# Four Strassen pairs per feed-forward in place of three, a longer lead, and plain weights split in one piece

## The chip, the cores and the metric

The kernel runs on one core of a Trainium2 chip. The metric is the device time of one execution in microseconds (us), as a median over runs. TensorE (PE) multiplies matrices, VectorE (DVE) and ScalarE (ACT) work element by element, GpSimd (POOL) takes small side jobs, and SyncE (SP) issues the transfers from device memory.

## The reference, cut to what matters

The program runs two transformer blocks of depth 2, one after the other, over a sequence of 256 tokens of width 1024 in float32. Each of the four layers has a feed-forward, a token mixer and another feed-forward, so there are eight feed-forwards:

```
def swiglu(x, w13, w2):                      # D_FF = 2816
    a, b = jnp.split(x @ w13, 2, axis=-1)
    return (jax.nn.silu(a) * b) @ w2

def swiglu_2(h, w_in, w_out):
    gu = h @ w_in
    g, u = jnp.split(gu, 2, axis=-1)
    return (jax.nn.silu(g) * u) @ w_out
```

The first block puts layer norms around feed-forwards and mixer (`x = layer_norm(ALPHA * x + 0.5 * swiglu(...))`), the second RMS norms. The mixers (gated recurrence and spatial gating in the first block, dilated attention and mLSTM in the second) are not touched by the change, but their weights pass through the same splitting code.

## The kernel before, in words

**Precision.** A float32 matrix is written as the sum of two reduced-precision matrices: a high part, which is a copy that rounds (ScalarE, line 268), and a low part, which is the matrix less its high part (VectorE, line 274; for 14 halves GpSimd, line 272). A product takes three matmuls: high by high, high by low, low by high (`mm3`, line 302, and line 547 in the pairs). `wh` and `wl` are the parts of a weight, `xh` and `xl` those of the activations.

**Units.** All weights come as one stream of units of 128 x 1024 numbers. A plain unit is loaded into the pool `stg` (four buffers) and split in two halves of 512 columns, each with one copy and one subtraction. `split(u)` splits all units up to number `u`, and `fetch` issues loads up to four units (`STAGES`) further. How far splitting runs ahead of TensorE's use in the order of the program is `lead()`: 2 to 5 units for plain ones, `PAIR` units where a product unit comes within `PAIR` units. A unit's two parts, and the loaded blocks of a pair, live in one ring of 24 buffers (`whp`, 2 x `RING`).

**The feed-forward.** The 2816 hidden columns are 11 groups of 256 (each group is one 512-column product: gate and value side by side), and the second matrix has 22 rows of units (`r`). The two halves of the tokens (i = 0 and 1) first do two groups (`OWN`) each by themselves. Then comes the joint part, in which every unit serves both halves (`joint`, the list `FFN`): `("g", n)` is one plain group, `("s", n, ...)` a pair of groups n and n + 1 by Strassen's products, with the rows named behind it done in the gaps, and `("r", k)` a row alone. After it each half does the six rows in `LAST`, and the norm follows.

**A pair.** Two groups by both token halves are a 2 x 2 block product. `pair` does it with seven products instead of eight. It loads four blocks in two units each (`raw`, lines 232 and 233). Seven operands are made from them, partly by adding blocks in place (`operand`, lines 245, 249 and 253, VectorE), and each operand is split 1024 columns at a time. On the way out of a pair ScalarE keeps four products (line 501), VectorE adds them (line 504) and multiplies by the gate (line 511), and the hidden rows are transposed and split (lines 294 and 295). A plain group instead ends in `hidden` (lines 440 to 451, 256 columns at a time).

**Order.** The order of instructions on TensorE, VectorE and ScalarE is set by a scheduler of the framework from the order of the program and its dependencies; SyncE and GpSimd keep the order of the program. Each engine works strictly in its order.

Of the kernel before, what the change touches and what calls it, by code (L numbers as in the profile page):

```python
# [11 lines left out]
F32 = mybir.dt.float32  # L12
# [7 lines left out]
P = 128  # L20
# [16 lines left out]
RAMP = 3  # L37
STEP = 1
TAIL = 2
PAIR = 5  # L40
LAGS = dict(ffn=9, mixer1=6, mixer2=6)
STAGES = 4
SLOTS = 31
# [10 lines left out]


OWN = 2
FFN = (("g", 8), ("s", 2, 0, 1, 2, 3), ("g", 9), ("s", 4, 16, 17, 4, 5), ("g", 10), ("s", 6, 6, 7, 18, 19),
       ("r", 8), ("r", 9), ("r", 20), ("r", 21))
LAST = (10, 11, 12, 13, 14, 15)


PRODUCTS = ("p1", "p2", "q5", "p3", "p6", "p7", "q4")
# [16 lines left out]
class Core:  # L79
# [125 lines left out]
    def lead(self):  # L205
# [3 lines left out]
        left = dict(ffn=len(_ffn_units()), mixer1=56, mixer2=36)[kind] - n  # L209
        if self.product(min(self.pos[0] + PAIR, self.nunit - 1)):  # L210
            return PAIR
        return LEAD + (MORE if n < FIRST else max(0, MORE - left // RAMP))
# [11 lines left out]
    def fetch(self, v):  # L224
        while self.next_dma <= min(v, self.nunit - 1):
            made = self.made[self.next_dma]
            if not self.product(self.next_dma):
                t = self.stages[self.next_dma] = self.stg.tile([P, 1024], F32, tag="stg", name=self.nm("stg"))
                for c in (slice(0, 512), slice(512, 1024)) if self.next_dma == 0 else (slice(0, 1024),):
                    self.nc.sync.dma_start(t[:, c], self.a["ws"][made][:, c])  # L230
            elif made[0] in LOADS:
                t = self.raw[made[:2]] = self.whp.tile([P, 1024], F32, tag="w", name=self.nm("raw"))
                self.nc.sync.dma_start(t, self.block(LOADS[made[0]], *made[1:]))
            self.next_dma += 1

# [3 lines left out]
    def operand(self, p, u, base):  # L239


        raw, add = self.raw, self.nc.vector.tensor_add
        if p in ("q5", "p6"):
            t = raw["p1", u]
            add(t, t, raw["q5" if p == "q5" else "p3", u])  # L245
            return t
        if p == "p7":
            t = raw.pop(("p3", u))
            add(t, t, raw.pop(("q5", u)))  # L249
            return t  # L250
        if p == "q4":
            t = raw.pop(("p1", u))
            add(t, t, raw.pop(("p2", u)))  # L253
            return t
        return raw[p, u]

    def split(self, u):
        while self.next_split <= min(u, self.nunit - 1):
            v = self.next_split
            self.fetch(v)  # L260
            made = self.made[v]
            product = self.product(v)
            w = self.operand(*made) if product else self.stages.pop(v)
            hi = self.whp.tile([P, 1024], F32R, tag="w", name=self.nm("wh"))
            lo = self.whp.tile([P, 1024], F32R, tag="w", name=self.nm("wl"))
            halves = [slice(0, 512), slice(512, 1024)]
            for h, c in enumerate([slice(0, 1024)] if product else halves):
                r = self.nc.scalar.activation(hi[:, c], w[:, c], AF.Copy)  # L268
                if v < 3:
                    self.pin(r)  # L270
                if h and self.pool_share(*self.phase[v]):
                    self.nc.gpsimd.tensor_tensor(lo[:, c], w[:, c], hi[:, c], op=ALU.subtract)
                else:
                    self.nc.vector.tensor_sub(lo[:, c], w[:, c], hi[:, c])  # L274
            self.units[v] = [hi[:, c] for c in halves], [lo[:, c] for c in halves]
            self.next_split += 1
            self.fetch(v + STAGES)
# [135 lines left out]
    def ffn(self, i, rs):  # L413
# [16 lines left out]
        while "done" not in J:  # L430
            yield 1
        yield from self.rows(i, range(len(LAST)), lambda n: J["h", i, LAST[n]], accs, None, len(LAST) - 1)
        return accs
# [23 lines left out]
    def joint(self, J, rs):  # L457

        for what, n, *ks in FFN:
            if what == "s":  # L460
# [1001 lines left out]
def _ffn_units():  # L1462


    out, n = list(range(4 * OWN)), 4 * OWN
    for what, _, *ks in FFN:
        if what == "s":
            base, gaps = n, GAPS[len(GAPS) - len(ks):]
            n += 8
            for p in PRODUCTS:  # L1470
                out += [(p, u, base) for u in range(2)]
                if p in gaps:
                    out.append(n)
                    n += 1
        else:
            m = 4 if what == "g" else 1
            out += range(n, n + m)
            n += m
    return out + list(range(n, n + len(LAST)))

# [15 lines left out]
def _ffn(w_in, w_out):  # L1496
    groups, w_out = _pairs(w_in), _rows(w_out)
    parts = [groups[:4 * OWN]]
    for what, n, *ks in FFN:
        if what == "s":  # L1500
            parts += [_blocks(w_in, n), w_out[list(ks)]]
        else:
            parts.append(groups[4 * n:4 * n + 4] if what == "g" else w_out[n:n + 1])
    return parts + [w_out[list(LAST)]]

# [94 lines left out]
```

## Time and profile before

| | before |
|---|---|
| median of 3 runs | 2171.57 us (2169.29 to 2174.26) |
| profiled execution | 2170.61 us, its span 2168.8 us |
| TensorE busy | 2116.2 us, 98% of the span |
| VectorE busy | 1879.8 us, 87% |
| ScalarE busy | 1352.0 us, 62% |
| GpSimd busy | 291.4 us, 13% |
| read from device memory | 391.63 MB, 181 GB/s over the span |

The span runs from the first instruction's start to the last one's end. Busy times are unions, so what overlaps on one engine counts once. Matmuls are pipelined and their ends are modelled: the rate of TensorE is better read from the starts of matmuls in a row than from its busy time.

### The profile page before, as it was taken

How to read it: one execution, taken by the hardware profiler on the slowest of the kernel's cores; microseconds unless marked ns; L12 is line 12 of the kernel's file. 1: busy time of each engine (PE TensorE's matmuls, PEld its weight loads, DVE VectorE, ACT ScalarE, POOL GpSimd, SP SyncE). 2: the span in 40 equal slices, each digit the busy share in tenths (PEclk: the TensorE clock that was granted, in tenths of full speed). 3: DMA queues.
4: the chain of work that ended last, by engine and by line, in shares of the span. 5: the costliest groups of instructions: out<-in, count | busy, mean ns of one | idle time of the engine just before them, and what ended most of it. 6: DMA issues, size and time to landing. Idle time of an engine off the chain costs nothing.

```text
span 2168.8 us, 28670 instructions
## 1 busy us (share of the span) xinstructions
PE 2116.2 (98%) x9968; PEld 1738.6 (80%) x9968; DVE 1879.8 (87%) x2837; ACT 1352.0 (62%) x2351; POOL 291.4 (13%) x319
## 2 busy tenths in 40 slices
PE   8999999999999999999999999999999999999998
PEld 6877888888788788888778787788778878788887
DVE  7998787899889879698989988689998998877995
ACT  6665755566566575565656665666666666576663
POOL 0000420000000033000100304610200010550000
PEclk9999999999999999999999999999999999999999
DMA  8547455455654655545555553434655546343552
GB/s 301 185 176 244 148 190 193 141 213 201 208 190 175 218 160 180 178 159 197 199 197 203 204 194 122 165 117 148 233 195 186 182 172 219 111 152 127 205 192 97
DMA packets 115296, 394.55 MB, mean 182 GB/s; under 512 B 12880, under 2 KB 15312, under 8 KB 115152
## 3 DMA queue, kind: packets, MB, share of 16 engines
q1 hardware_dynamic: 115152, 392.73, 52.5%
q8 instruction: 78, 1.28, 0.2%
q14 instruction: 66, 0.54, 0.1%
HBM read 391.63 MB, written 1.05 MB: 181 GB/s over the span
## 4 chain that ended last, share of the span: by engine, by line
PE 80%; DVE 10%; issue 3%; ACT 3%; POOL 2%; DMA 2%; SPq 0%; DVEq 0%; POOLq 0%; ACTq 0%
PE g L302 33%; PE big L302 23%; PE g L547 17%; DVE wl L274 5%; PE g L286 4%; ACT wh L268 2%; DMA stg<-in_ws_dram 2%; PE big L1262 1%; PE big L1291 1%; PE big L792 1%; DVE raw L245 1%; DVE kp L504 0%; DVE raw L249 0%; PE big L1209 0%; POOL cu L1135 0%
## 5 line engine op out<-in xcount | busy, mean ns | idle before, releaser
L274 DVE TENSOR_TENSOR wl<-stg,wh 128x512 fp32r<-128x512 f32 x1026 | 691.8, 708 | 129.6 <-ACT wh L268 123.3
L268 ACT ACTIVATE wh<-stg 128x512 fp32r<-128x512 f32 x1040 | 600.8, 623 | 200.8 <-PE g L302 83.8
L302 PE MATMUL g<-wh,xh 128*128 128x512 f32 x1184 | 483.1, 408 | 9.3 <-ACT wh L268 5.9
L302 PE MATMUL g<-wl,xh 128*128 128x512 f32 x1184 | 467.2, 395 | 0.5 <-DVE wl L274 0.5
L302 PE MATMUL g<-wh,xl 128*128 128x512 f32 x1184 | 465.3, 395 | 0.0
L268 ACT ACTIVATE wh<-raw 128x1024 fp32r<-128x1024 f32 x336 | 349.3, 1056 | 178.1 <-DVE raw L253 53.7
L274 DVE TENSOR_TENSOR wl<-raw,wh 128x1024 fp32r<-128x1024 f32 x336 | 410.2, 1236 | 25.1 <-ACT wh L268 23.1
L302 PEld LDWEIGHTS g<-wh,xh 128*128 128x128 f32 x1184 | 225.5, 190 | 58.8 <-ACT wh L268 7.3
L302 PEld LDWEIGHTS g<-wh,xl 128*128 128x128 f32 x1184 | 224.7, 190 | 50.4 <-DVE xl L311 2.0
L302 PEld LDWEIGHTS g<-wl,xh 128*128 128x128 f32 x1184 | 225.7, 191 | 43.4 <-DVE wl L274 1.8
L302 PE MATMUL big<-wh,hT 128*128 128x512 f32 x640 | 183.3, 390 | 0.0
L547 PE MATMUL g<-wh,Xh 128*128 128x512 f32 x384 | 149.7, 390 | 1.1 <-ACT kp L501 1.1
L547 PE MATMUL g<-wl,Xh 128*128 128x512 f32 x384 | 150.7, 393 | 0.0
L547 PE MATMUL g<-wh,Xl 128*128 128x512 f32 x384 | 150.2, 391 | 0.0
L302 PEld LDWEIGHTS big<-wh,hT 128*128 128x128 f32 x640 | 120.1, 188 | 25.3
L410 POOL TENSOR_TENSOR m<-m,nhalf 128x1 f32<-128x1 f32 (+1 forms) x24 | 23.1, 962 | 794.5 <-DVE m L409 794.5
L302 PE MATMUL big<-wh,hTh 128*128 128x512 f32 x384 | 124.8, 392 | 0.0
L302 PE MATMUL big<-wl,hTh 128*128 128x512 f32 x384 | 124.2, 390 | 0.0
L302 PE MATMUL big<-wh,hTl 128*128 128x512 f32 x384 | 124.0, 390 | 0.0
L245 DVE TENSOR_TENSOR raw<-raw,raw 128x1024 f32<-128x1024 f32 x96 | 120.6, 1268 | 0.5
L547 PE MATMUL g<-wh,xh 128*128 128x512 f32 x288 | 114.6, 398 | 1.4 <-ACT kp L501 1.4
L547 PE MATMUL g<-wl,xh 128*128 128x512 f32 x288 | 112.5, 391 | 0.0
(322 smaller groups left out, 3229.2 us busy)
## 6 DMA issues: line engine op xcount, KB each, us to landing
stg<-in_ws_dram SPq DMA_DIRECT2D x519, 512.0 KB, 4.4
raw<-in_ws_dram SPq DMA_DIRECT2D x192, 512.0 KB, 5.0
row<-in_norm_gain_dram SPq DMA_DIRECT2D x24, 256.0 KB, 6.8
row<-in_ln_g_dram SPq DMA_DIRECT2D x12, 256.0 KB, 4.9
row<-in_ln_b_dram SPq DMA_DIRECT2D x12, 256.0 KB, 6.3
xT<-in_xT_dram SPq DMA_DIRECT2D x4, 256.0 KB, 6.1
x<-in_x_dram SPq DMA_DIRECT2D x4, 256.0 KB, 8.7
out_dram<-x SPq DMA_DIRECT2D x4, 256.0 KB, 2.0
```

What stands on the lines that cost most here:

```text
L245: add(t, t, raw["q5" if p == "q5" else "p3", u])
L268: r = self.nc.scalar.activation(hi[:, c], w[:, c], AF.Copy)
L274: self.nc.vector.tensor_sub(lo[:, c], w[:, c], hi[:, c])
L286: self.nc.tensor.transpose(tp[:, hs(j)], src[:, hs(j)], self.ident)
L302: self.nc.tensor.matmul(accs[c], a, b[c], start=start and q == 0, stop=stop and q == 2)
L410: self.nc.gpsimd.tensor_tensor(out, out, self.nhalf[:, 0:n], op=ALU.pow)
L547: nc.tensor.matmul(bank[p], x[:, hs(k)], w[j], start=first[p] == p and k + q == 0, stop=k == 3 and q == 2, skip_group_check=True)
L792: nc.tensor.matmul(ps[:, 64 * h:64 * h + 64].rearrange("p (c m) -> p c m", m=m), Z[:, hs(h)], view(Z[:, hs(h)], m)[:, :, 1, :], start=True ...
L1262: nc.tensor.matmul(ps[:, hh * S + j * P:hh * S + j * P + P], J["aq", i][r, hs(head // 2)], J["ak", j][r, hs(head // 2)], start=True, stop= ...
L1291: nc.tensor.matmul(o[:, 64 * hh:64 * hh + 64], pT[:, hs(2 * hh + j)], J["av", j][:, head * 64:head * 64 + 64], start=j == 0, stop=j == 1)
```

## The change

Three edits. First, the list `FFN` has one plain group and four pairs one behind the other, where it had three groups and three pairs in turn; the rows are dealt out anew, and because two pairs now overlap in the stream, the loaded blocks are kept under a key with the pair's position (`base`) in it. Second, `PAIR` is 6 in place of 5. Third, a plain unit from number 8 on is split in one piece of 1024 columns, except the 14 units in the second mixers whose second half GpSimd splits.

```diff
-PAIR = 5
+PAIR = 6
...
-FFN = (("g", 8), ("s", 2, 0, 1, 2, 3), ("g", 9), ("s", 4, 16, 17, 4, 5), ("g", 10), ("s", 6, 6, 7, 18, 19),
-       ("r", 8), ("r", 9), ("r", 20), ("r", 21))
-LAST = (10, 11, 12, 13, 14, 15)
+FFN = (("g", 10), ("s", 2, 0, 1, 2, 3), ("s", 4, 20, 21, 4, 5), ("s", 6, 6, 7, 8, 9), ("s", 8, 10, 11, 12),
+       ("r", 13))
+LAST = (14, 15, 16, 17, 18, 19)
...
-                t = self.raw[made[:2]] = self.whp.tile([P, 1024], F32, tag="w", name=self.nm("raw"))
+                t = self.raw[made] = self.whp.tile([P, 1024], F32, tag="w", name=self.nm("raw"))
...
         if p in ("q5", "p6"):
-            t = raw["p1", u]
-            add(t, t, raw["q5" if p == "q5" else "p3", u])
+            t = raw["p1", u, base]
+            add(t, t, raw["q5" if p == "q5" else "p3", u, base])
             return t
...
-            for h, c in enumerate([slice(0, 1024)] if product else halves):
+            for h, c in enumerate([slice(0, 1024)] if product or v >= 8 and not self.pool_share(*self.phase[v]) else halves):
```

In the whole program the matmuls of 512 columns go from 8256 to 8160, the 1024-wide low parts of operands from 336 to 448, the operand sums from 192 to 256, and the low parts of plain units from 1026 instructions of 512 columns to 434 of 1024 and 30 of 512.

VectorE's order changes most behind a pair. This is VectorE before, in the third feed-forward, behind the last low part of its first pair; `stg` names a plain unit, `raw` a block or operand of a pair, `kp6` and `kp7` are kept products:

```order
L504 TENSOR_TENSOR kp6_1352_5721<-kp6_1352_5721,g_1334_5630 128x512
L274 TENSOR_TENSOR wl_1366_5789<-stg_1345_5686,wh_1365_5788 128x512
L511 SCALAR_TENSOR_TENSOR kp6_1352_5721<-kp6_1352_5721,kp1_1323_5580 128x512
L274 TENSOR_TENSOR wl_1366_5789<-stg_1345_5686,wh_1365_5788 128x512
L295 TENSOR_TENSOR hTl_1359_5750<-g_1357_5744,hTh_1358_5749 128x512
L504 TENSOR_TENSOR kp7_1364_5773<-kp7_1364_5773,kq5_1338_5650 128x512
L274 TENSOR_TENSOR wl_1369_5803<-stg_1348_5706,wh_1368_5802 128x512 x2
L274 TENSOR_TENSOR wl_1372_5811<-stg_1351_5713,wh_1371_5810 128x512 x2
L274 TENSOR_TENSOR wl_1377_5828<-stg_1356_5730,wh_1376_5827 128x512 x2
L511 SCALAR_TENSOR_TENSOR kp7_1364_5773<-kp7_1364_5773,sg_1374_5824 128x512
```

And this is VectorE now, at the same place:

```order
L274 TENSOR_TENSOR wl_1374_5471<-raw_1361_5420,wh_1373_5470 128x1024
L504 TENSOR_TENSOR kp6_1371_5466<-kp6_1371_5466,g_1353_5379 128x512
L274 TENSOR_TENSOR wl_1384_5506<-raw_1364_5438,wh_1383_5505 128x1024
L511 SCALAR_TENSOR_TENSOR kp6_1371_5466<-kp6_1371_5466,kp1_1339_5324 128x512
L295 TENSOR_TENSOR hTl_1378_5494<-g_1376_5488,hTh_1377_5493 128x512
L504 TENSOR_TENSOR kp7_1386_5523<-kp7_1386_5523,kq5_1354_5392 128x512
L274 TENSOR_TENSOR wl_1388_5527<-stg_1367_5445,wh_1387_5526 128x1024
L274 TENSOR_TENSOR wl_1391_5533<-raw_1370_5458,wh_1390_5532 128x1024
L274 TENSOR_TENSOR wl_1394_5551<-raw_1375_5474,wh_1393_5550 128x1024
L245 TENSOR_TENSOR raw_1361_5420<-raw_1361_5420,raw_1385_5509 128x1024
L511 SCALAR_TENSOR_TENSOR kp7_1386_5523<-kp7_1386_5523,sg_1399_5575 128x512
L245 TENSOR_TENSOR raw_1364_5438<-raw_1364_5438,raw_1389_5530 128x1024
```

Where the units of the next plain group stood between the pair's last steps, operands of the next pair and two of its sums stand now.

TensorE's order changes there too. Before, at the end of that pair, the last product (line 547, `wh_1354` is its second unit) is followed by the next plain group (line 302):

```order
L547 MATMUL g_1316_5550<-wh_1354_5726,xh_95 128x512
L547 MATMUL g_1316_5550<-wl_1355_5727,xh_95 128x512
L547 MATMUL g_1316_5550<-wh_1354_5726,xl_96 128x512
L302 MATMUL g_1385_5847<-wh_1365_5788,xh_95 128x512
L302 MATMUL g_1385_5847<-wl_1366_5789,xh_95 128x512
L302 MATMUL g_1385_5847<-wh_1365_5788,xl_96 128x512
```

Now, at the seam between the second and the third pair, the bank `g_1467` takes the third pair's first product and `g_1403` the second pair's last:

```order
L286 MATMUL g_1444_5769<-con_94,kp6_1439_5747 128x128 x4
L547 MATMUL g_1467_5856<-wh_1441_5751,xh_95 128x512
L547 MATMUL g_1467_5856<-wl_1442_5752,xh_95 128x512
...
L547 MATMUL g_1467_5856<-wh_1447_5778,xh_95 128x512
L547 MATMUL g_1467_5856<-wl_1448_5779,xh_95 128x512
L547 MATMUL g_1403_5583<-wh_1433_5722,xh_95 128x512
L547 MATMUL g_1403_5583<-wl_1434_5723,xh_95 128x512
L547 MATMUL g_1403_5583<-wh_1433_5722,xl_96 128x512
```

The next pair's first product has moved ahead of this pair's last one.

## Rows read from the trace of the kernel before

**Rows 1.** The page: busy time of TensorE and VectorE, and TensorE's granted clock.

```profile
PE 2116.2 (98%) x9968; PEld 1738.6 (80%) x9968; DVE 1879.8 (87%) x2837; ACT 1352.0 (62%) x2351; POOL 291.4 (13%) x319
...
PEclk9999999999999999999999999999999999999999
```

**Rows 2.** The page: chain that ended last, by engine and by line.

```profile
PE 80%; DVE 10%; issue 3%; ACT 3%; POOL 2%; DMA 2%; SPq 0%; DVEq 0%; POOLq 0%; ACTq 0%
PE g L302 33%; PE big L302 23%; PE g L547 17%; DVE wl L274 5%; PE g L286 4%; ACT wh L268 2%; DMA stg<-in_ws_dram 2%; PE big L1262 1%; PE big L1291 1%; PE big L792 1%; DVE raw L245 1%; DVE kp L504 0%; DVE raw L249 0%; PE big L1209 0%; POOL cu L1135 0%
```

**Rows 3.** Stretches, the eight joint parts: length, then each engine's busy time (instructions).

```profile
core 0: us, PE busy (x) PEld busy (x) DVE busy (x) ACT busy (x) POOL busy (x), PEclk, DMA share, GB/s
...
578.00:722.00 144.00, 143.99 (x654) 118.59 (x653) 132.43 (x166) 91.78 (x144) 0.00 (x0) 1.00 0.56 196
...
1133.00:1280.00 147.00, 143.43 (x647) 117.11 (x648) 140.58 (x175) 97.08 (x149) 16.98 (x7) 1.00 0.56 196
...
sum 1154.00, PE 1139.40 PEld 934.13 DVE 1085.64 ACT 753.64 POOL 53.31; mean PE 142.43 PEld 116.77 DVE 135.70 ACT 94.21 POOL 6.66
```

**Rows 4.** Chain in order of time, inside a pair: start, length (us), what.

```profile
601.79 5.44 PE g L547 x24
```

**Rows 5.** Timeline of VectorE in a pair: start, length (us), line, operation, count [idle before].

```profile
604.75 0.68 DVE L504 TENSOR_TENSOR kp<-kp,g 128x512 f32<-128x512 f32 x1
605.35 1.22 DVE L274 TENSOR_TENSOR wl<-raw,wh 128x1024 fp32r<-128x1024 f32 x1
606.48 1.29 DVE L274 TENSOR_TENSOR wl<-stg,wh 128x512 fp32r<-128x512 f32 x2
607.69 1.22 DVE L253 TENSOR_TENSOR raw<-raw,raw 128x1024 f32<-128x1024 f32 x1
608.82 2.35 DVE L274 TENSOR_TENSOR wl<-raw,wh 128x1024 fp32r<-128x1024 f32 x2
611.09 1.28 DVE L274 TENSOR_TENSOR wl<-stg,wh 128x512 fp32r<-128x512 f32 x2
...
615.86 1.23 DVE L274 TENSOR_TENSOR wl<-raw,wh 128x1024 fp32r<-128x1024 f32 x1 [1.21 <-ACT wh L268]
...
641.46 0.75 DVE L451 TENSOR_TENSOR hT<-g,hT 128x256 fp32r<-128x256 f32 x2
```

**Rows 6.** Stretches of 16 us behind seven joint parts (the last rows): sum.

```profile
sum 112.00, PE 111.77 PEld 92.33 DVE 89.54 ACT 71.66 POOL 1.70; mean PE 15.97 PEld 13.19 DVE 12.79 ACT 10.24 POOL 0.24
```

**Rows 7.** Timeline of ScalarE in a pair: copies of halves and of whole units.

```profile
622.04 3.22 ACT L268 ACTIVATE wh<-stg 128x512 fp32r<-128x512 f32 x6
...
627.48 2.00 ACT L268 ACTIVATE wh<-raw 128x1024 fp32r<-128x1024 f32 x2
```

**Rows 8.** Stretches, the four mixers (from 206, 756, 1297 and 1825): sum.

```profile
sum 733.00, PE 719.36 PEld 597.88 DVE 571.52 ACT 444.55 POOL 220.67; mean PE 179.84 PEld 149.47 DVE 142.88 ACT 111.14 POOL 55.17
```

**Rows 9.** The page: costliest groups, the low parts of weights (busy us, mean ns).

```profile
L274 DVE TENSOR_TENSOR wl<-stg,wh 128x512 fp32r<-128x512 f32 x1026 | 691.8, 708 | 129.6 <-ACT wh L268 123.3
...
L274 DVE TENSOR_TENSOR wl<-raw,wh 128x1024 fp32r<-128x1024 f32 x336 | 410.2, 1236 | 25.1 <-ACT wh L268 23.1
```

**Rows 10.** Stretches: one pair without a gap on TensorE, and one with.

```profile
638.10:669.00 30.90, 30.90 (x141) 25.55 (x140) 30.73 (x38) 20.58 (x33) 0.00 (x0) 1.00 0.36 125
1718.50:1752.20 33.70, 31.41 (x141) 25.41 (x140) 32.49 (x37) 22.17 (x34) 5.96 (x4) 1.00 0.56 202
```

**Rows 11.** Timeline of TensorE in the second of these pairs.

```profile
1741.99 0.50 PE L547 MATMUL g<-wh,Xh 128*128 128x512 f32 x1 [1.07 <-ACT kp L501]
...
1744.66 0.63 PE L286 MATMUL g<-con,kp 128*128 128x128 f32 x4 [1.22 <-DVE kp L511]
```

**Rows 12.** The page: DMA issues of the pairs' blocks (KB each, us to landing).

```profile
raw<-in_ws_dram SPq DMA_DIRECT2D x192, 512.0 KB, 5.0
```

More of the change, by code (lines that the diff above doesn't have):

```diff
@@ L243, in operand @@
         if p in ("q5", "p6"):
-            t = raw["p1", u]
-            add(t, t, raw["q5" if p == "q5" else "p3", u])
+            t = raw["p1", u, base]
+            add(t, t, raw["q5" if p == "q5" else "p3", u, base])
             return t
         if p == "p7":
-            t = raw.pop(("p3", u))
-            add(t, t, raw.pop(("q5", u)))
+            t = raw.pop(("p3", u, base))
+            add(t, t, raw.pop(("q5", u, base)))
             return t
         if p == "q4":
-            t = raw.pop(("p1", u))
-            add(t, t, raw.pop(("p2", u)))
+            t = raw.pop(("p1", u, base))
+            add(t, t, raw.pop(("p2", u, base)))
             return t
-        return raw[p, u]
+        return raw[p, u, base]
     def split(self, u):
```

## The prediction

> **What bounds the kernel now.** I read the page's busy lines and the chain of waits first. TensorE is busy 2116.2 us of the span, VectorE 1879.8 us, and TensorE's granted clock is at its upper level (2.4 GHz) in every slice [rows 1]; the chain runs 80% of the span over TensorE and 10% over VectorE [rows 2]. So TensorE sets the end, with VectorE close behind. That is an average. The change sits in the joint part of each feed-forward (pairs, groups and rows that serve both token halves), so I then cut the trace into the eight joint parts. In the 144 us from 578 on, TensorE has 143.99 us of work and VectorE 132.4; in the 147 us from 1133 on, TensorE 143.4 and VectorE 140.6. All eight together last 1154.0 us, with 1139.4 us of TensorE and 1085.6 us of VectorE: 68.4 us of free VectorE time, 8.5 us for each [rows 3]. That number decides the case.
>
> **What the change takes from TensorE.** A pair of Strassen products is 7 x 2 x 2 x 3 = 84 matmuls of 512 columns, the two plain groups that it replaces are 2 x 48 = 96. One pair more in each of eight feed-forwards saves 8 x 12 = 96 matmuls. 24 of them in a row take 5.44 us [rows 4], 0.227 us each, so 96 are 21.8 us (2.7 us for each feed-forward). The transposes stay the same in number. If TensorE stayed the bound, that would be the result.
>
> **What it puts on VectorE.** Not durations but spacings count, since instructions overlap a little. In an unbroken run a 512-wide one follows the one before after 0.60 us (604.75 to 605.35); a plain unit split in two halves holds the engine 1.21 us (606.48 to 607.69); a 1024-wide instruction holds it 1.135 us (two from 608.82 to 611.09); two of 256 columns take 0.75 us [rows 5]. Each feed-forward gets one more pair: 14 low parts and 8 operand sums, 22 x 1.135 = 25.0 us, and 7 instructions of 512 columns (three adds, two products, two low parts of the transposed hidden rows), 7 x 0.60 = 4.2 us; together 29.2 us. It loses two plain groups: 8 units x 1.21 = 9.7 us and 8 instructions of 256 columns, 3.0 us. The 20 plain units that stay in a joint part (one group, 16 rows) are split in one piece: 20 x (1.21 - 1.135) = 1.5 us less. Net +15.0 us of VectorE for each joint part, against 8.5 us that are free and a TensorE time that shrinks by 2.7 us. Over eight: 1085.6 + 120.0 = 1205.6 us of VectorE in stretches that lasted 1154.0. Where the old order puts four plain units, with their cheap 1.21 us, behind each pair, the new one has the next pair's units and sums there, as the two pieces of VectorE's order show. So the bound changes engine, and the joint parts grow by 51.6 us if VectorE never waits and no work of it moves out of them.
>
> **What stands on either side of 51.6.** First, VectorE does wait. In the present pairs it stands 1.21 us for ScalarE's copy of the last product, with nothing to do between sum and low part [rows 5]. In the new order both of these sums stand together and cover each other's copies, so I take 0.5 us a pair: 32 x 0.5 = +16; ends 0 and 32 x 1.21 = +39. Second, work can be left for later. When the last product is done TensorE still has a row and the six last rows, and in these stretches VectorE is now idle 112.0 - 89.5 = 22.5 us over seven of them [rows 6], 3.2 us each: 8 x 3.2 = -26, which I take whole; ends 0 and -26. Third, the 434 - 160 = 274 wide splits outside the joint parts free 274 x 0.075 = 20.6 us of VectorE, and on ScalarE a wide copy takes 2.00 / 2 = 1.00 us where two halves take 3.22 / 3 = 1.07 [rows 7]. In the four mixers TensorE is busy 719.4 of 733.0 us [rows 8], so at most 13.6 us could come back; against it, the first half of a unit now comes 1.135 - 0.60 = 0.5 us later. I take -5; ends -14 and +5. The sixth unit of lead costs no instruction. It can put one cheap unit (1.135 us) more in hand before the pairs, 8 x 1.135 = -9 at best; I take 0, since a lead that VectorE can't refill is spent once. ScalarE gets 14 more copies of 1.00 us a joint part and loses 16 halves; it is nowhere near its limit. DMA moves the same bytes.
>
> Sum: 51.6 + 16 - 26 - 5 = +36.6 us on the profiled execution's 2170.6, so 2207; the median shown lies 1 us above that execution, so **2208 us**.
>
> **A rule of the Trainium skill against this.** VectorE's spacing rows say that a wide split saves 0.075 us. By the mean durations of the groups it would be 2 x 0.708 - 1.236 = 0.18 us [rows 9]. "VectorE: DVE Perf Modes" (section "The TRN2 errata") says that each instruction with its operands in SBUF pays a fixed latency, once for a large tile and again for every small one, which is a reason for the second reading. By it the joint parts would get 160 x 0.105 = 17 us back; the spacing rows of this trace do not agree, so the sum goes by 0.075.
>
> **Rivals.**
> (a) TensorE stays the bound: faster. Then -21.8 for the matmuls and -5 for the wide splits: 2145 us. For it: TensorE has no gap in the stretch from 578 on, and VectorE there is free for 144 - 132.4 = 11.6 us [rows 3], so that units split ahead might carry the pairs through. Against it: six units in hand are some 6 x 1.135 = 7 us, once, where a joint part lacks 15.0 - 8.5 + 2.7 = 9 us. It decides only if VectorE's additions measure under 8.5 us. Chance 0.12.
> (b) No wait of VectorE at all, the wide split worth 0.18 us as by the durations [rows 9], the sixth unit of lead worth its whole 9 us and the mixers unmoved: 51.6 + 0 - 26 - 17 - 9 = 0, no change, 2172 us. Chance 0.08.
> (c) Lock-step: slower by more. TensorE's order has the next pair's first product ahead of the last product of this one, and ScalarE's kept sums wait for TensorE while the copies of later units are queued behind them. In one pair of today this is seen: 33.70 us in place of 30.90 [rows 10], TensorE idle 1.07 us for ScalarE's kept product and 1.22 us for VectorE's hidden row [rows 11]. If each of 32 pairs lost these 2.3 us on top, in place of my 16: +36.6 - 16 + 73 = +94, 2265 us. It decides where VectorE is idle over 2 us a pair. Chance 0.12.
> (d) The lead isn't there: the ring of 24 buffers holds eight loaded blocks and two buffers for each split unit, so the next pair's blocks may be loaded only when this pair's end. A block lands 5.0 us after its issue [rows 12]; bare at each of 24 seams between pairs that is 120 us on the time before, 2292 us at worst. Against it: a VectorE that is late leaves few split units in the ring. Chance 0.04.
> The forecast has 0.64.
>
> **How the numbers follow.** About 0.2% (4.3 us) is what a measurement of this kernel tells from no change. Faster by more than that is (a) and a little of the forecast's low tail: 0.13. Within it is (b), less its tails: 0.06. Slower: 0.81. The forecast's own range, from its three bounded terms half way to their ends, is 2190 to 2235. For 8 in 10 it goes down to 2168, which takes in (b), and up to 2250, part of (c).
>
> **What would show it.** In the changed profile: TensorE's matmul count 96 lower, but its busy time stretched or its gaps grown inside the pairs; VectorE busy near 1879.8 + 120 - 21 = 1979 us and over 97% in the joint parts; the step from one pair's start to the next near VectorE's 26 x 1.135 + 7 x 0.60 = 33.7 us (four plain rows with it) where TensorE's 132 matmuls and the transposes need 30.9 [rows 10]; joint parts some 4 to 7 us longer each; the mixers unchanged within a few us. It is wrong if the pairs follow each other at 31 us, if VectorE stands idle over 2 us a pair, or if the mixers move more than the joint parts.

## The result, and the profile after

The changed kernel takes 2250.85 us (median of 4 runs, 2250.79 to 2251.44) against 2170.83 us (2169.29 to 2174.26): ratio 1.037, 95% interval 1.0357 to 1.0383. It is 80 us slower. The forecast was 2208 us, slower by 37; the measurement lies above the forecast's own range (2190 to 2235 us) and just above its wider one (up to 2250). The direction and the engine were right, the size was not.

The page of the changed kernel, beside [rows 1, 2]:

```profile
PE 2128.3 (95%) x9872; PEld 1728.8 (77%) x9872; DVE 1978.8 (88%) x2443; ACT 1366.3 (61%) x1901; POOL 294.0 (13%) x319
...
DVE  7998787899899868699999998579999998777997
...
PE 57%; DVE 24%; issue 8%; DMA 5%; ACT 4%; POOL 2%; DVEq 0%; SPq 0%; POOLq 0%; ACTq 0%
PE g L302 23%; PE g L547 14%; PE big L302 13%; DVE wl L274 12%; DMA stg<-in_ws_dram 5%; PE g L286 3%; DVE raw L245 2%; ACT wh L268 2%; DVE kp L504 1%; DVE kp L511 1%; DVE raw L249 1%; POOL cu L1135 1%; DVE raw L253 1%; PE big L1262 1%; DMA raw<-in_ws_dram 1%
```

VectorE is busy 1978.8 us (forecast 1979), 96 matmuls are gone, and VectorE's share of the chain went from 10% to 24%. TensorE's busy time rose by 12 us although it has less to do, so I count the time that its 512-column matmuls don't cover, each at the 0.227 us of an unbroken run [rows 4].

Stretches of the changed kernel from the first product of a feed-forward's first pair to the end of its last pair, as in [rows 3]; four of the eight, and the sum of all:

```profile
422.90:556.80 133.90, 128.88 (x568) 104.01 (x568) 129.05 (x127) 86.31 (x103) 0.00 (x0) 0.99 0.52 175
616.40:750.30 133.90, 128.88 (x567) 103.84 (x567) 128.94 (x127) 85.84 (x103) 0.00 (x0) 0.99 0.51 174
1192.60:1327.50 134.90, 128.57 (x567) 103.85 (x566) 133.66 (x127) 86.29 (x103) 11.03 (x6) 0.99 0.50 175
...
1547.20:1682.50 135.30, 128.50 (x567) 103.82 (x566) 134.01 (x127) 86.27 (x103) 11.05 (x6) 0.99 0.49 170
...
sum 1076.10, PE 1025.64 PEld 826.01 DVE 1053.50 ACT 695.11 POOL 42.05; mean PE 128.21 PEld 103.25 DVE 131.69 ACT 86.89 POOL 5.26
```

and the sum of the same eight stretches of the kernel before:

```profile
sum 944.20, PE 930.53 PEld 763.11 DVE 902.33 ACT 625.86 POOL 52.40; mean PE 116.32 PEld 95.39 DVE 112.79 ACT 78.23 POOL 6.55
```

VectorE is busy 1053.50 of 1076.10 us, 98%, and idle for 22.6 us in place of 41.9: it sets the pace there. The same cut through every kernel gives the account of this study. "Pairs" are these eight stretches; the rest is split into the three seams from one feed-forward to the next, the first block's two mixers, the second block's two mixers (each with the rows, norms and plain groups on both sides of it), and what lies at both ends (start and end, about 20 everywhere, not listed). Each row comes from one profiled execution, and executions of one kernel lie a few us apart. Time not covered by 512-column matmuls, us:

| kernel | ratio | pairs | seams | first mixers | second mixers | all outside pairs |
|---|---|---|---|---|---|---|
| before | 1 | 48.1 | 20.3 | 76.3 | 129.7 | 246.6 |
| after | 1.037 | 106.1 | 36.7 | 85.4 | 150.0 | 291.1 |
| four_halves | 1.0325 | 107.1 | 33.9 | 77.3 | 142.6 | 274.3 |
| four_wffn | 1.0308 | 105.6 | 33.3 | 75.7 | 142.1 | 271.7 |
| four_tail | 1.0414 | 156.2 | 21.6 | 72.8 | 136.4 | 251.8 |
| four_twosums | 0.9973 | 49.1 | 29.4 | 76.7 | 141.8 | 266.8 |
| four_nosums | 0.9935 | 37.9 | 20.4 | 74.7 | 146.7 | 261.5 |
| w_only | 1.0083 | 47.5 | 18.5 | 80.0 | 140.0 | 257.9 |

For the changed kernel: +58.0 in the pairs, +44.5 outside, -21.8 for the matmuls saved (96 x 0.227) is +80.7, the difference of the two profiled spans (2249.6 and 2168.8 us).

Three pairs of the changed kernel, start to start (columns as above):

```profile
616.40:647.40 31.00, 31.00 (x141) 25.34 (x141) 28.48 (x30) 20.24 (x25) 0.00 (x0) 1.00 0.53 190
680.00:714.10 34.10, 32.01 (x141) 25.40 (x140) 33.86 (x35) 22.07 (x26) 0.00 (x0) 1.00 0.56 183
1254.50:1291.40 36.90, 32.50 (x142) 25.26 (x141) 36.90 (x33) 22.41 (x26) 5.92 (x4) 1.00 0.58 204
```

The first pair of a feed-forward still runs at TensorE's 31.0 us (32.0 in the very first), the second takes 30.9 to 32.6 (35.6 there). From the third on the reserve is spent (but for the last feed-forward's third, 32.1): 34.1 us where VectorE alone sets the step (forecast 33.7), 36.9 where GpSimd works beside it. Inside the third of these, VectorE's timeline has no idle time, and TensorE waits for it:

```profile
1264.71 1.21 DVE L245 TENSOR_TENSOR raw<-raw,raw 128x1024 f32<-128x1024 f32 x1
1265.84 1.22 DVE L274 TENSOR_TENSOR wl<-raw,wh 128x1024 fp32r<-128x1024 f32 x1
1266.98 1.22 DVE L274 TENSOR_TENSOR wl<-stg,wh 128x1024 fp32r<-128x1024 f32 x1
1268.11 2.35 DVE L274 TENSOR_TENSOR wl<-raw,wh 128x1024 fp32r<-128x1024 f32 x2
```

```profile
1260.88 0.66 PE L286 MATMUL g<-con,kp 128*128 128x128 f32 x4 [1.22 <-DVE kp L511]
...
1267.11 0.50 PE L547 MATMUL g<-wl,Xh 128*128 128x512 f32 x1 [0.79 <-DVE wl L274]
...
1277.30 0.50 PE L547 MATMUL g<-wl,Xh 128*128 128x512 f32 x1 [0.86 <-DVE wl L274]
```

The low part that ends at 1267.06 (1265.84 + 1.22) releases the matmul at 1267.11. No one wait is long; TensorE's waits of the changed kernel show how many there are (line waited for: us in total, times, longest us):

```profile
PE g L286 <- DVE kp L511: 33.3, 28, 2.0
PE g L286 <- DVE x L593: 18.4, 9, 3.6
PE g L547 <- DVE wl L274: 17.9, 28, 1.1
PE g L302 <- POOL wl L272: 13.7, 2, 6.8
```

The first and third are the pairs. The second and fourth stand behind them: at the norms, and in the second mixers.

### The profile page after: what moved, and what is told of

Same layout as the page of the kernel before. It is cut to its first block, busy times and chain, and to the rows that moved or that the text cites. A ratio compares the mean times of both kernels' runs of the same rounds, so it can differ in the third digit from the quotient of the medians.

```text
span 2249.6 us, 27649 instructions
## 1 busy us (share of the span) xinstructions
PE 2128.3 (95%) x9872; PEld 1728.8 (77%) x9872; DVE 1978.8 (88%) x2443; ACT 1366.3 (61%) x1901; POOL 294.0 (13%) x319
## 4 chain that ended last, share of the span: by engine, by line
PE 57%; DVE 24%; issue 8%; DMA 5%; ACT 4%; POOL 2%; DVEq 0%; SPq 0%; POOLq 0%; ACTq 0%
PE g L302 23%; PE g L547 14%; PE big L302 13%; DVE wl L274 12%; DMA stg<-in_ws_dram 5%; PE g L286 3%; DVE raw L245 2%; ACT wh L268 2%; DVE kp L504 1%; DVE kp L511 1%; DVE raw L249 1%; POOL cu L1135 1%; DVE raw L253 1%; PE big L1262 1%; DMA raw<-in_ws_dram 1%
## 5 line engine op out<-in xcount | busy, mean ns | idle before, releaser
L274 DVE TENSOR_TENSOR wl<-stg,wh 128x1024 fp32r<-128x1024 f32 (+1 forms) x464 | 566.1, 1227 | 114.8 <-ACT wh L268 111.1
L268 ACT ACTIVATE wh<-stg 128x1024 fp32r<-128x1024 f32 (+1 forms) x478 | 480.3, 1015 | 197.4 <-DMA stg<-in_ws_dram 75.6
L268 ACT ACTIVATE wh<-raw 128x1024 fp32r<-128x1024 f32 x448 | 464.2, 1056 | 179.0 <-DVE raw L245 69.9
L274 DVE TENSOR_TENSOR wl<-raw,wh 128x1024 fp32r<-128x1024 f32 x448 | 547.2, 1239 | 14.7 <-ACT wh L268 12.9
L302 PE MATMUL g<-wh,xh 128*128 128x512 f32 x928 | 383.4, 413 | 8.9 <-ACT wh L268 5.8
L302 PE MATMUL g<-wl,xh 128*128 128x512 f32 x928 | 370.1, 399 | 13.7 <-POOL wl L272 13.7
L302 PE MATMUL g<-wh,xl 128*128 128x512 f32 x928 | 369.9, 400 | 6.3 <-DVE xl L311 6.3
L302 PEld LDWEIGHTS g<-wh,xl 128*128 128x128 f32 x928 | 178.5, 192 | 48.1 <-DVE xl L311 9.9
L547 PE MATMUL g<-wl,Xh 128*128 128x512 f32 x512 | 201.8, 394 | 12.3 <-DVE wl L274 12.1
L547 PE MATMUL g<-wh,Xh 128*128 128x512 f32 x512 | 200.2, 391 | 0.0
L547 PE MATMUL g<-wl,xh 128*128 128x512 f32 x384 | 153.5, 400 | 5.8 <-DVE wl L274 5.8
L547 PE MATMUL g<-wh,xh 128*128 128x512 f32 x384 | 154.3, 404 | 0.0
L547 PE MATMUL g<-wh,xl 128*128 128x512 f32 x384 | 152.0, 398 | 0.0
L547 PEld LDWEIGHTS g<-wl,Xh 128*128 128x128 f32 x512 | 96.1, 188 | 39.6 <-DVE wl L274 20.5
```

The source lines that it names most:

```text
L302: self.nc.tensor.matmul(accs[c], a, b[c], start=start and q == 0, stop=stop and q == 2)
L547: nc.tensor.matmul(bank[p], x[:, hs(k)], w[j], start=first[p] == p and k + q == 0, stop=k == 3 and q == 2, skip_group_check=True)
```

## Experiments

My theory: VectorE has too much work in the pairs (A). Rivals: the wide split costs the time (B), the sixth unit of lead or the ring does (C), and lock-step between the engines, which needs VectorE idle inside the pairs. VectorE's idle time in the four pairs of a feed-forward together is 1.1 to 5.0 us (length less busy time in the stretches above), so lock-step fell by the profile alone. So did rival (d) of the prediction, bare loads at the seams between pairs: all waits of the program that the trace puts down to the load of a pair's block come to 0.3 us. Ratios are to the kernel before on the same chip, with 95% intervals.

**Each part alone.** The kernel before with the wide split only (w_only):

```diff
-            for h, c in enumerate([slice(0, 1024)] if product else halves):
+            for h, c in enumerate([slice(0, 1024)] if product or v >= 8 and not self.pool_share(*self.phase[v]) else halves):
```

> The kernel before with the third edit alone: plain units split 1024 columns at a time, three pairs, lead 5. Theory A (the joint parts are short of VectorE, and all that is lost outside them follows from units that arrive late): VectorE loses about 33 us of work, so the pairs that GpSimd slows shrink a little; 2160 to 2172 us. Theory B (the wide split itself does harm outside the joint parts, by later halves and by holding GpSimd up in the second mixers): 2185 to 2205 us, with TensorE waiting some 7 us in each second mixer for GpSimd's low halves.

1.0083 (1.0065 to 1.0101), 18 us: the wide split is a loss, not the gain of 5 I had taken. The changed kernel with that line undone (four_halves):

> The changed kernel with plain units split in halves again: four pairs, lead 6. Theory A: VectorE gets 33 us more, about 13 of them in the joint parts, so the time stays or grows: 2250 to 2270 us. Theory B: what is lost outside the joint parts comes back: 2210 to 2230 us.

1.0325 (1.0309 to 1.0341), which lies between the two expectations. By the ratios the wide split is some 10 of the 80 us, and four pairs with the longer lead are the rest. The lead, with `PAIR = 5` in the changed kernel (four_lead5) and `PAIR = 6` in the one before (lead6_only):

> The changed kernel with lead 5 in pairs in place of 6. Theories A and B: the lead is used up in the first pairs and not refilled, 2245 to 2262 us. Theory C (the sixth unit of lead fills the ring of 24 buffers and holds up the loads of the next pair): 2210 to 2235 us.

> The kernel before with the second edit alone, lead 6 in pairs. Where plain groups lie between the pairs VectorE refills its lead, so one unit more should do little on any theory: 2158 to 2172 us. If the ring of 24 buffers were what binds, later loads would show: 2175 us or more.

1.0436 (1.0418 to 1.0454) and 1.0042 (1.0029 to 1.0056). By the ratios the sixth unit helps four pairs by 14 us (by the medians 11), so theory C fell for the changed kernel. In the kernel before it costs 9. Why is open: 2178.77 us lies where a ring that binds was expected (2175 us or more), and no run parts that from other causes.

**Is it VectorE?** The changed kernel without its 256 operand sums (four_nosums: `operand` returns a raw block instead; what it computes is not the reference's product):

```diff
-            t = raw["p1", u, base]
-            add(t, t, raw["q5" if p == "q5" else "p3", u, base])
-            return t
+            return raw["p1", u, base]
```

> The changed kernel without the 256 operand sums of 1024 columns on VectorE: each product takes a loaded block as it is, so that the output isn't the reference's; all loads, copies, low parts and matmuls stay. It takes 256 x 1.135 = 291 us off VectorE, all in the pairs. Theory A: the four pairs follow each other at 31 us each, the joint parts give back their 57 us and the stretches behind them most of their loss; 2140 to 2165 us. Theory B: the joint parts give back 57 us, but the loss outside stays: 2185 to 2200 us.

0.9935 (0.992 to 0.995), VectorE busy 1707.9 us. Its second feed-forward's first and last pair, by stretches:

```profile
408.30:439.20 30.90, 30.90 (x141) 25.44 (x140) 21.03 (x22) 18.56 (x23) 0.00 (x0) 1.00 0.59 202
500.70:528.60 27.90, 27.90 (x128) 23.00 (x127) 25.36 (x26) 21.38 (x27) 0.00 (x0) 1.00 0.58 206
```

TensorE runs without a gap at its own 30.9 us: with VectorE relieved, four pairs do what they were written for. Outside the pairs 14.9 of the 44.5 us stay (this kernel keeps the wide split), and the second mixers keep all of theirs and more, 17.0 us: that part doesn't come from VectorE's work in the pairs. How much relief that takes, from four_halves without the sums of one operand (four_onesum, 64 instructions) and of two (four_twosums, 128):

```diff
-            add(t, t, raw.pop(("q5", u, base)))
+            raw.pop(("q5", u, base))
...
-            add(t, t, raw.pop(("p2", u, base)))
+            raw.pop(("p2", u, base))
```

> Four pairs with lead 6 and split halves, without the sums for the seventh product (64 instructions, 64 x 1.135 = 73 us of VectorE; the operand is a loaded block, so that the output isn't the reference's). Theory A (VectorE's work in the joint parts sets the time one for one until TensorE binds): about 60 to 73 us less than four pairs with all sums, ratio to the kernel before 0.998 to 1.006, 2165 to 2185 us. Rival (order and waits, not work, cost the time): less than 30 us of gain, ratio above 1.018.

> The same without the sums for the sixth and the seventh product (128 instructions, 145 us of VectorE; again not the reference's output). Theory A: the first 74 us or so count one for one, the rest finds TensorE the bound, so little more than with one: ratio 0.990 to 0.998, 2150 to 2168 us. Rival: the gain goes on in proportion to the work, ratio 0.97.

1.0079 (1.0054 to 1.0103) and 0.9973 (0.9961 to 0.9985). The first 73 us of VectorE (64 x 1.135) bring 53 us, a little less than theory A's 60 to 73, and the next 73 bring 23. By a straight line between the two, four pairs break even when VectorE is spared about 130 us. Giving the same two sums to GpSimd is the version that keeps the result (four_poolsums; `self.nc.gpsimd.tensor_tensor(..., op=ALU.add)` for these two `add`):

> Four pairs with lead 6 and split halves, with 128 of the 256 operand sums (those for the sixth and seventh products) on GpSimd in place of VectorE: 145 us off VectorE. Theory A with both engines side by side: the pairs come down to 31 to 32 us each, 2170 to 2195 us. Rival (the two engines get in each other's way, as where a low part of 1.22 us took 1.99 beside GpSimd): little or nothing is won, 2230 us or more.

1.1096 (1.107 to 1.1122). GpSimd's operations, and VectorE's beside them, in one pair:

```profile
705.30 3.18 POOL L249 TENSOR_TENSOR raw<-raw,raw 128x1024 f32<-128x1024 f32 x1 [1.30 <-PE big L302]
708.44 6.15 POOL L253 TENSOR_TENSOR raw<-raw,raw 128x1024 f32<-128x1024 f32 x2
```

```profile
701.79 3.30 DVE L245 TENSOR_TENSOR raw<-raw,raw 128x1024 f32<-128x1024 f32 x1
705.01 4.56 DVE L274 TENSOR_TENSOR wl<-raw,wh 128x1024 fp32r<-128x1024 f32 x2
709.49 5.64 DVE L274 TENSOR_TENSOR wl<-stg,wh 128x512 fp32r<-128x512 f32 x2
```

A sum takes GpSimd 3.1 us, and VectorE is held up meanwhile: two low parts take 4.56 us where they take 2.35 alone, two halves 5.64 where they take 1.29 [rows 5]. The Trainium skill states this in "SBUF — State Buffer" (section "SBUF: two separate sides"): for instructions of VectorE with two inputs in SBUF, as these are, the two engines share a pair of ports as an exclusive lock, and while one has it the other is blocked. The trace agrees that VectorE is held up beside GpSimd's sums (4.56 us in place of 2.35); how the lock passes between them it doesn't show.

**What is lost behind the pairs.** Behind the second feed-forward, TensorE of the changed kernel:

```profile
572.35 0.39 PE L302 MATMUL big<-wh,hTl 128*128 128x512 f32 x1
576.10 0.66 PE L286 MATMUL g<-con,x 128*128 128x128 f32 x4 [3.36 <-DVE x L593]
578.65 1.09 PE L286 MATMUL g<-con,x 128*128 128x128 f32 x4 [1.90 <-DVE x L593]
```

and VectorE just ahead of it, with the norm's steps (lines 592 and 593) queued between low parts of the next units:

```profile
570.86 1.17 DVE L274 TENSOR_TENSOR wl<-stg,wh 128x1024 fp32r<-128x1024 f32 x1
571.95 0.14 DVE L409 TENSOR_SCALAR m<-m 128x1 f32<-128x1 f32 x1
572.01 0.74 DVE L592 SCALAR_TENSOR_TENSOR t<-t,m,row 128x512 f32<-128x512 f32 x1
574.15 1.23 DVE L274 TENSOR_TENSOR wl<-stg,wh 128x1024 fp32r<-128x1024 f32 x1 [1.40 <-ACT wh L268]
575.30 0.74 DVE L593 SCALAR_TENSOR_TENSOR x<-t,m,row 128x512 f32<-128x512 f32 x1
```

VectorE has idle time here (1.40 us), but it is waiting in order for a copy while the norm's second step, which TensorE needs, stands behind the low part. The copy in turn waits for its unit. This is the chain of waits that ended last, at the same place (start, length in us, what):

```profile
565.63 1.15 DVE wl L274
566.79 6.17 DMA stg<-in_ws_dram
...
573.06 1.06 ACT wh L268
...
575.30 0.74 DVE x L593
```

A low part of VectorE sets one of the four buffers of plain units free, only then does the load of a later unit start (SyncE's twelve issues from 550 to 575 us waited 18.0 us for low parts), and its copy and low part stand ahead of the norm's step. Added up over the three seams, such loads are 26.0 us of the chain here and 25.4 in four_twosums, against 13.3 in the kernel before, 6.2 in four_tail (below) and 4.4 in four_nosums: the seams are long where loads stand on the chain. Whether more buffers would help, no run tests. To give VectorE more room behind the last pair, four_halves with its plain group and two rows more put there (four_tail):

```diff
-FFN = (("g", 10), ("s", 2, 0, 1, 2, 3), ("s", 4, 20, 21, 4, 5), ("s", 6, 6, 7, 8, 9), ("s", 8, 10, 11, 12),
-       ("r", 13))
-LAST = (14, 15, 16, 17, 18, 19)
+FFN = (("s", 2, 0, 1, 2, 3), ("s", 4, 4, 5), ("s", 6, 6, 7, 8, 9), ("s", 8, 10, 11, 12), ("g", 10),
+       ("r", 13), ("r", 14), ("r", 15))
+LAST = (16, 17, 18, 19, 20, 21)
```

> Four pairs with lead 6 and split halves, but with the plain group and two rows more behind the pairs in place of ahead of them: the same work in another order. Theory D (some 28 us are lost behind the joint parts, because VectorE arrives late at the last rows and the norm): the group gives VectorE time to catch up, ratio to the kernel before about 1.02, 2205 to 2222 us. Rival (the same shortage is only moved, and the first pair now starts with less in hand): ratio 1.03 to 1.04, 2230 to 2250 us.

1.0414 (1.0394 to 1.0434), slower than even the rival had it. The seams did recover (33.9 to 21.6): that loss is one of room behind the last pair. It isn't only work carried over from the pairs, since four_twosums, whose pairs run almost as freely as those before, keeps 29.4 there. But the pairs lost 49 us more, with VectorE idle for 0.1 to 0.3 us in each of the eight stretches: the shortage moved.

**Where the wide split loses.** Three kernels: the wide split in the feed-forwards only, in the kernel before (w_ffn_only) and in the changed one (four_wffn), and w_only with no low half on GpSimd (w_nopool):

```diff
-            for h, c in enumerate([slice(0, 1024)] if product else halves):
+            for h, c in enumerate([slice(0, 1024)] if product or v >= 8 and self.phase[v][0] == "ffn" else halves):
```

```diff
-        return kind == "mixer2" and 8 <= n < 28 and n % 3 == 2
+        return False
```

> The kernel before with the wide split in the feed-forwards alone; the mixers keep halves. If the wide split's loss sits in the mixers (late low halves on GpSimd and around them): ratio 0.996 to 1.001, 2160 to 2174 us. If it sits at the norms and first groups, where a first half is waited for: ratio 1.004 to 1.009.

> The changed kernel with the wide split kept for the plain units of the feed-forwards only; mixers and the rest are split in halves as before. Theory (the wide split costs its time in the mixers): the time is that of the changed kernel with halves everywhere, ratio 1.031 to 1.034, 2238 to 2244 us, TensorE's time outside the pairs 274 to 278 us. Rival (with VectorE late behind every joint part, a first half that comes 0.5 us later is paid in the feed-forwards too): ratio 1.035 to 1.037, 290 us outside the pairs.

> The kernel before with the wide split, and with the 14 low halves of GpSimd in the second mixers given to VectorE (so those units are split in one piece too). Theory B1 (the wide split loses its time by TensorE's waits of some 7 us in each second mixer for those low halves): 2155 to 2172 us, the waits gone. Theory B2 (it loses it because halves come later everywhere): 2178 to 2192 us.

1.0008 (0.9996 to 1.0019), 1.0308 (1.029 to 1.0325) and 1.0024 (1.0012 to 1.0037). In the feed-forwards the wide split costs nothing, so its whole loss is in the mixers, and in w_only most of it goes when GpSimd has no low halves (the second mixers go from 140.0 to 134.1 us). That pointed to GpSimd; so did the changed kernel, where TensorE waits 6.8 us in each second mixer for one. Two tests of that follow: four_halves with the same `return False` (four_halves_nopool), and the fourth part of the convolution moved from GpSimd to VectorE, in four_wffn (four_vconv) and in the kernel before (vconv):

```diff
-        side = self.start(part(3, nc.gpsimd, CP))
+        side = self.start(part(3, nc.vector, CP))
```

> The changed kernel with halves everywhere and with no low half on GpSimd: VectorE takes those 14 halves itself, 14 x 0.60 = 8.4 us in two mixers. Theory (GpSimd late beside a busy VectorE makes TensorE wait some 7 us in each second mixer): 10 to 14 us faster than with them, ratio 1.026 to 1.028. Rival (the lateness is VectorE's own, GpSimd only shows it): the wait goes over to VectorE's low parts, ratio 1.031 to 1.034, unchanged.

> The changed kernel with the wide split in the feed-forwards only and the same four parts of the convolutions on VectorE. Theory (one operation of GpSimd that is held for 6.2 us beside VectorE's run makes everything behind it late, whichever that is: a low half, or the rotation of a key when no half is there): TensorE's waits for GpSimd in the second mixers (7.6 us here once, 14 with halves everywhere) fall under 3 us together; ratio 1.026 to 1.029 against 1.031 without this edit. Rival (GpSimd is late because VectorE hands it its inputs late): the waits stay, 1.030 to 1.032.

> The kernel before with the fourth part of each convolution of the two second mixers on VectorE (five instructions of some 0.4 us) in place of GpSimd (nine of 0.7 to 1.1 us): four parts, 8 us more of VectorE. Theory (the two engines stretch each other in the convolution: in the kernel before VectorE's eight instructions of it took 5.70 us, 3.22 in the changed kernel): VectorE's eight fall to 3.2 us, TensorE's wait of 2.9 us for the gates in each second mixer gets shorter; ratio 0.996 to 1.000. Rival (the wait is the late convolution itself, whoever computes it): 1.000 to 1.003.

1.031 (1.0293 to 1.0326), 1.0306 (1.0293 to 1.032) and 1.0014 (1.0004 to 1.0024): no change that these runs can tell in the changed kernel, a small loss in the one before. My theory fell both times. TensorE's longest wait in the second block's first mixer, in four_halves, four_halves_nopool and four_vconv:

```profile
1396.88 0.80 PE L302 MATMUL g<-wl,xh 128*128 128x512 f32 x1 [7.21 <-POOL wl L272]
```

```profile
1402.48 1.12 PE L286 MATMUL g<-con,ak 128*128 128x128 f32 x4 [5.00 <-POOL ak L1024]
```

```profile
1395.70 0.69 PE L286 MATMUL g<-con,ak 128*128 128x128 f32 x2 [4.61 <-POOL vx L1005]
```

Whatever is taken from GpSimd, what it does next is late. Its timeline there, in four_halves and then in four_vconv, shows it held up:

```profile
1383.10 6.17 POOL L1135 TENSOR_SCALAR cu<-cv,prm 128x254 f32<-128x254 f32 x1
...
1390.98 2.56 POOL L1135 TENSOR_SCALAR cu<-cv,prm 128x255 f32<-128x255 f32 x1
```

```profile
1391.72 1.14 POOL L1021 TENSOR_TENSOR rw<-ak,con 128x64 f32<-128x64 f32 x1
1392.82 2.15 POOL L1022 TENSOR_TENSOR rw<-ak,con 128x64 f32<-128x64 f32 x1
```

Where they are not held up, line 1135 takes 0.95 us (kernel before) and lines 1021 and 1022 take 0.32 (changed kernel). VectorE runs its own convolution beside them; its eight instructions in the kernel before, and in four_halves:

```profile
1343.99 5.70 DVE L1133 SCALAR_TENSOR_TENSOR qk<-cv,prm,qk 128x254 f32<-128x254 f32 x8
```

```profile
1383.19 3.22 DVE L1133 SCALAR_TENSOR_TENSOR qk<-cv,prm,qk 128x254 f32<-128x254 f32 x8
```

In the kernel before VectorE gave way and GpSimd's step took 0.95 us; in four_halves VectorE ran through and GpSimd's took 6.17. What decides who gives way the runs don't tell. That the second mixers lose 13 us in four_halves is measured; how much of it is this, and how much VectorE's order around it, stays open. It isn't the doing of four pairs alone: TensorE waits 13.7 us for these low halves in w_only, with three pairs, and not at all in four_tail, with four.

**A cost that moves.** The norm gains of the second block are multiplied on GpSimd inside the pairs, and stretch VectorE there ([rows 10], the pair with 5.96 us of GpSimd). The kernel before with `ahead(94, ...)` for `ahead(60, ...)` (gains_late) has them later:

> The kernel before with GpSimd's products of the norm gains, in the feed-forwards of the second block, moved from the pairs to the rows behind them (34 steps of the program later), nothing else. Theory E (in the joint parts VectorE is so near its limit that GpSimd's few operations there, which slow it, cost the 3 to 4 us by which those joint parts are longer): about -10 us, ratio 0.993 to 0.997. Rival (they cost as much where they go, or come too late for the norm): ratio 0.999 to 1.004.

1.003 (1.0019 to 1.0041). They landed in the last pair and not behind it, so the edit did not do what it was for: the last pair's length went from 32.6 to 35.7 us while the second step fell from 44.1 to 42.5 (fifth feed-forward).

## Why the prediction was too low

- **Matmuls saved, -21.8.** Right: 9968 matmuls became 9872, and four_nosums shows them gained once VectorE is out of the way.
- **VectorE's work, 15.0 us more for each joint part.** Right: 1978.8 us busy against 1979 forecast, 98% in the pairs against over 97%, 34.1 us for a third pair against 33.7. Rival (a) is refuted by this and by four_onesum and four_twosums, which get faster as VectorE gets less.
- **VectorE's waits, +16 (0.5 us a pair).** About right: 22.6 us over 32 pairs, 0.7 a pair. Rival (c) needed over 2.
- **Work left for the last rows, -26.** This step failed. The prediction let late work go behind the pairs at no price; the stretches behind them got longer by 27.7 us. In full, four_halves has 59.0 us more in the pairs and 27.7 behind them, 86.7 together, where my terms give 51.6 + 16 - 26 + 21.8 = 63 in the same units and 89 without the credit. I read VectorE's idle time behind the pairs [rows 6] as room for late work. It was idle by its order, waiting for copies, and already in the kernel before the copies wait there for loads: 21.0 us over the seven stretches. ScalarE's waits in one of them, from 722 to 738 (line waited for: us in total, times, longest us):

```profile
ACT wh L268 <- DMA stg<-in_ws_dram: 3.9, 4, 2.0
```

The last pair now also has one row behind it in the joint part in place of four. Of the 27.7 us 13.6 are in the seams, where the loads stand on the chain, and 12.9 in the second mixers, where TensorE waits 14.4 us for GpSimd's low halves and did not wait for them before; no term had that. Late work alone is not shown to be the cause: four_twosums, whose pairs are about as free as before, keeps 20.2 of the 27.7.
- **Wide split, -5 (ends -14 and +5).** This step failed too: +18 alone, and in the changed kernel a ratio of 1.037 against 1.0308 and 1.0325 with the mixers in halves, some 10 to 13 us. I had seen that the first half of a unit comes 0.5 us later and let VectorE's saving outweigh it. In the mixers VectorE is not what is short (690 of 886 us busy in the stretches around them in the changed kernel), so its saving finds no use there; most of the loss goes when GpSimd has no low halves (w_nopool, 1.0024). In the feed-forwards the net is nothing (1.0008).
- **A rule against the trace.** By "VectorE: DVE Perf Modes" of the Trainium skill (section "The TRN2 errata") one wide instruction saves a fixed latency. By durations I had put it at 0.18 us a unit, against the 0.075 of the spacings that my sum used. VectorE's busy time in w_only is 1849.4 us in place of 1879.8 for 498 such units, 0.061 us each: the saving is there, and it is nearer to the spacings.
- **Sixth unit of lead, 0 (end -9).** Right in sign of the end, too small: it is worth 11 to 14 us to four pairs.
- **Mixers unchanged within a few us.** Wrong: +9.1 and +20.3.

With the credit at 0 and the wide split at +10 to +13 the sum is 78 to 81, against 80 measured. That is closer than the account deserves: the sixth unit's 11 to 14 us, which it takes at 0, and the second mixers' 12.9 us, which it doesn't have, happen to cancel. The range, too, was not quite what it was said to be: half way to the ends of the three terms is some 2195 to 2238 us, which the measurement misses as well. Neither failed step touches the choice of the engine; both credited a saving without asking what would use it, and for the first the profile of before held the answer in ScalarE's waits.

## What to carry to other kernels

Idle time of an engine that works in a fixed order is room only for work that can be placed in it: look at what the idle instruction waits for, and at what stands behind it, before crediting it. Here an engine with 6% free got more work than that, and neither another order of it (four_tail) nor a shorter lead (four_lead5) won anything back; taking work off it did, 130 us to break even. The wider instruction cost nothing where that engine was short, and lost time in the mixers, where it wasn't.

## What the hardware showed

**VectorE and GpSimd.** GpSimd's 0.95 us step was held for 6.17 us while VectorE ran more than eight instructions without a gap, and in the pair shown of four_poolsums VectorE's 1.2 us low parts took twice as long (over the whole kernel a mean of 1.45 us in place of 1.23). So GpSimd, though 87% idle, was no place for 145 us of VectorE's work.

**TensorE's clock.** The granted clock falls to the lower level (1.2 GHz) at some of TensorE's waits and stays there for a while behind them. Three stretches of the changed kernel: in a pair, behind a wait of 1.97 us that ended at 718.98; at the norm behind the second feed-forward (waits of 3.36 and 1.90 us, shown above); and around the wait of 6.84 us for GpSimd that ended at 1407.12:

```profile
720.20:723.60 3.40, 3.40 (x10) 2.63 (x9) 3.40 (x4) 3.39 (x5) 0.00 (x0) 0.50 0.00 0
576.80:583.60 6.80, 4.95 (x14) 4.11 (x15) 6.80 (x9) 4.16 (x6) 0.00 (x0) 0.50 0.75 297
1402.90:1413.10 10.20, 5.98 (x16) 4.82 (x17) 3.97 (x6) 2.57 (x5) 9.86 (x14) 0.50 0.29 104
```

Matmuls at the end of the second one, and the first at full speed behind it:

```profile
582.09 0.63 PE L302 MATMUL g<-wh,xh 128*128 128x512 f32 x1
582.52 0.63 PE L302 MATMUL g<-wl,xh 128*128 128x512 f32 x1
...
583.74 0.40 PE L302 MATMUL g<-wl,xh 128*128 128x512 f32 x1
583.98 0.39 PE L302 MATMUL g<-wh,xl 128*128 128x512 f32 x1
```

They follow each other at 0.43 us in place of 0.23. The changed kernel has 12 such stretches with 64.9 us, the one before 4 with 20.5 (the end of the program left out); 105 and 35 wide matmuls run in them. So up to 70 x 0.20 = 14 us of the 80 are the waits' echo in the clock: less where VectorE was the bound anyway. They are part of the terms above and not one more.
